# An RWKV time-mixing kernel: crossbar transposes from an earlier unit, 16 KB loads, another queue for the first weight, and output matmuls one unit later

## The chip, the cores and the metric

The kernel runs on one core of one Trainium2 chip. The metric is the device time of one execution in microseconds. The kernel before took 206.17 us (median of three, 205.88 to 206.23). Only fast runs (the granted TensorE clock at or near full speed over most of the run) are compared. A ratio is the mean time of one kernel's fast runs over the mean of the other kernel's fast runs in the same rounds, so it is not quite the ratio of the medians quoted.

## The reference

```python
# x: (16, 2048, 256) float32; x_prev is x shifted by one position
xv = x * time_mix_v + x_prev * (1 - time_mix_v)
xr = x * time_mix_r + x_prev * (1 - time_mix_r)
v = xv @ value_weight
r = xr @ receptance_weight
out = (sigmoid(r) * v) @ output_weight      # the key branch does not reach the output
```

## The kernel before

A batch is 2048 rows; a unit is 512 rows, four units to a batch, 64 in all. x is loaded as bf16 (GpSimd's queue casts on the way), transposed (on TensorE for units below 49, by the transposing DMA, the "crossbar", from 49 on), mixed with its shifted neighbour on VectorE, GpSimd and later ScalarE, projected twice, gated and projected again. The parts that matter:

```python
    LOOK = 6
    BYDMA = 3 * UB + 3                # units transposed by the crossbar (UB = 4)
    CROSS = NU - BYDMA - LOOK         # 43: the pass in which the crossbar starts
    FREE = CROSS                      # from here ScalarE takes part of the scaling
    LATE_O = CROSS                    # from here output matmuls run one unit later
    xpool  = ctx.enter_context(tc.tile_pool(name="xpool", bufs=6))
    opool  = ctx.enter_context(tc.tile_pool(name="opool", bufs=3))   # output, one tile per batch
    ...
    def load(b):
        ...
        return nc.gpsimd.dma_start(out=x_bf[b], in_=rows(b), max_dma_last_dim=8192)

    x_unit = opool.tile([P, 3, UJ, D], FP32, name="o_sb")     # first three units of x, float32
    ...
    for m, tm in enumerate([time_mix_r, time_mix_v]):
        nc.scalar.dma_start(...)                              # the two mix vectors
    for h in (1, 0):
        nc.sync.dma_start(...)                                # two halves of unit 0 of x
    nc.sync.dma_start(out=w_f32[:, 0], ...)                   # first weight
    nc.sync.dma_start(out=x_unit[:, 1], ...)
    ...
    nc.gpsimd.tensor_copy(out=x_bf3[:, 0, 0:1], in_=w_f32[:, 0, 0, 0:1])   # a gate: loads wait for the weight
    ...
    def output(g, z):
        b, e = divmod(g, UB)
        if e == 0:
            o_sb[b] = opool.tile([P, J, D], FP32, name="o_sb")
        ...
        nc.scalar.copy(out=o_sb[b][:, j0 : j0 + UJ, :], in_=ps)
        if b < BYUNIT:
            if e % 2 == 1:
                nc.sync.dma_start(out=unit_rows(out, b, e - 1, 2), ...)    # two units, 4 KB runs
        elif e % 2 == 1:
            store(nc.sync, b, j0 - UJ, j0 + UJ)                            # two units, 8 KB runs
```

In the traces psum_r and psum_v are TensorE's result tiles of the two projections, psum_o that of the output matmuls, and ps_t that of the transposes; xt is the transposed x, s_sb the sigmoid, z_sb the gated product. Each of the first three has a single buffer.

There are three output tiles, and the first of them holds x at the start; so batch 4 writes into the tile of batch 1 and must wait until batch 1's stores have landed. And the loads of batches 2 to 6 are all issued ahead in the first 32 us, so many loads stand in GpSimd's DMA queue when the first stores are issued.

Of the kernel before, what the change touches and what calls it, by code (L numbers as in the profile page):

```python
# [15 lines left out]
def kernel(  # L16
# [25 lines left out]
    nc = tc.nc  # L42

    B, S, D = x.shape
    P = 128
    KO = D // P
    J = S // P
    UJ = 4
    TU = UJ * P
    UB = J // UJ  # L50
# [1 line left out]
    LOOK = 6  # L52
    BYUNIT = 2
    H = UJ // 2
    BYDMA = 3 * UB + 3
    CROSS = NU - BYDMA - LOOK
    FREE = CROSS
    LATE_O = CROSS
    START_T = [1, 3, 5, 6, 7, 9, 11, 12]
    AHEAD = 6  # L60
    PAIRS = 10
# [18 lines left out]
    x_bf = {}  # L80
# [12 lines left out]
    def rows(b):  # L93
        return x[b].rearrange("(p j) d -> p j d", p=P)

    def unit_rows(t, b, e, n=1):

        return t[b, e * TU : (e + n) * TU, :].rearrange("(e p j) d -> p e j d", p=P, j=UJ)

    def load(b):  # L100
        if b not in x_bf:
            x_bf[b] = xpool.tile([P, J, D], BF16, name="x_bf")
        if b < BYUNIT:
            for e in range(UB):
                nc.gpsimd.dma_start(  # L105
                    out=x_bf[b][:, e * UJ : (e + 1) * UJ, :], in_=unit_rows(x, b, e)[:, 0]
                )
            return
        return nc.gpsimd.dma_start(out=x_bf[b], in_=rows(b), max_dma_last_dim=8192)  # L109

    x_unit = opool.tile([P, 3, UJ, D], FP32, name="o_sb")
    tm_rows = consts.tile([2 * KO, P], FP32)
    w_f32 = consts.tile([P, 2, KO, D], FP32)
    for m, tm in enumerate([time_mix_r, time_mix_v]):
        nc.scalar.dma_start(
            out=tm_rows[m * KO : (m + 1) * KO, :], in_=tm.rearrange("(ko p) -> ko p", p=P)
        )
    for h in (1, 0):
        nc.sync.dma_start(
            out=x_unit[:, 0, h * H : (h + 1) * H], in_=unit_rows(x, 0, 0)[:, 0, h * H : (h + 1) * H, :]  # L120
        )
    nc.sync.dma_start(
        out=w_f32[:, 0], in_=receptance_weight.rearrange("(ko p) n -> p ko n", p=P)
    )
    nc.sync.dma_start(out=x_unit[:, 1], in_=unit_rows(x, 0, 1)[:, 0])
    nc.sync.dma_start(out=w_f32[:, 1], in_=value_weight.rearrange("(ko p) n -> p ko n", p=P))
    sig0 = consts.tile([P, 1], BF16)
# [4 lines left out]
    x_bf3 = consts.tile([P, UJ, D], BF16)  # L132
    nc.gpsimd.tensor_copy(out=x_unit[:, 2, 0, 0:1], in_=x_unit[:, 0, 0, 0:1])
    nc.sync.dma_start(out=x_unit[:, 2], in_=unit_rows(x, 0, 2)[:, 0])
    nc.gpsimd.tensor_copy(out=x_bf3[:, 0, 0:1], in_=w_f32[:, 0, 0, 0:1])
    nc.gpsimd.dma_start(out=x_bf3, in_=unit_rows(x, 0, 3)[:, 0])
    nc.gpsimd.dma_start(out=wo_bf, in_=output_weight.rearrange("(ko p) n -> p ko n", p=P))
    load(1)
# [40 lines left out]
    def by_dma(b, lo, hi, after=None):  # L179

        op = nc.sync.dma_start_transpose(
            out=xt[b][:, 1 + lo : 1 + hi].rearrange("p j k c -> p (j k) c"),
            in_=x_bf[b][:, lo:hi].rearrange("p j d -> p (j d)"),
        )
        if after is not None:
            tc.add_manual_dep(op.ins, after.ins.name, SYNC, reason="not beside a load")

    def transposes(i):

        b, e = divmod(i, UB)  # L190
        if b > 0 and e == 0:
            new_xt(b)
        if b >= BYUNIT:
            e = (e - 1) % UB
        j0 = 1 + e * UJ + (e if b < BYUNIT else 0)
        if b < BYUNIT or e == UB - 1:
            late_copies.append((b, e))

        def one(ps, jj, ko, src, idn):
            nc.tensor.transpose(  # L200
                out=ps[:, jj], in_=src[:, jj, ko * P : (ko + 1) * P], identity=idn
            )

        if i in (1, 2):
            for ko in range(KO):
                ps = ps_t_pool.tile([P, UJ, P], FP32, name="ps_t")
                for jj in range(UJ):
                    one(ps, jj, ko, x_unit[:, i], ident_f)
                nc.scalar.copy(out=xt[b][:, j0 : j0 + UJ, ko, :], in_=ps)
            return  # L210
        ps = ps_t_pool.tile([P, UJ, KO, P], BF16, name="ps_t")
        src = x_bf3 if b == 0 else x_bf[b][:, e * UJ : (e + 1) * UJ, :]
        for jj in range(UJ):
            for ko in range(KO):
                one(ps[:, :, ko], jj, ko, src, ident)
        nc.scalar.copy(out=xt[b][:, j0 : j0 + UJ], in_=ps)  # L216
# [70 lines left out]
    def project_unmixed(ps, mo):  # L287


        parts = [(w_prev[:, ko], ko, 0) for ko in range(KO)]  # L290
        parts += [(w_bf[:, 0, ko], ko, 1) for ko in range(KO)]
        for n, (w, ko, lo) in enumerate(parts):
            nc.tensor.matmul(
                out=ps[:, mo, :],
                lhsT=w[:, mo * P : (mo + 1) * P],
                rhs=xt[0][:, lo : lo + UJ, ko],
                start=(n == 0),
                stop=(n == len(parts) - 1),
            )
# [86 lines left out]
    def pieces(g):  # L386

        b, e = divmod(g, UB)
        tile_for(g // 2)
        return [(b, m, e * TU, (e + 1) * TU) for m in range(2)]  # L390
# [22 lines left out]
    last_load = None  # L413

    def advance(limit):
        nonlocal tnext, last_load
        while tnext <= min(limit, NU - 1):
            b, e = divmod(tnext, UB)
            if b == 1 and e > 0:
                load(b + e + 1)  # L420
            elif b > 1 and e == 0 and b + 5 < B:
                if b == 2:
                    load(6)
                last_load = load(b + 5)
            if tnext < NU - BYDMA:
                transposes(tnext)
            tnext += 1

    first_transposes()
    for ko in range(KO):  # L430
        nc.vector.tensor_scalar(
            out=w_prev[:, ko, :],
# [6 lines left out]
        out=w_bf[:, 0, 0, :], in0=w_f32[:, 0, 0, :], scalar1=tms[:, 0, 0:1], scalar2=None, op0=ALU.mult  # L439
    )  # L440
    nc.scalar.activation(
        out=w_bf[:, 0, 1, :], in_=w_f32[:, 0, 1, :], func=ACT.Copy, scale=tms[:, 0, 1:2]
# [3 lines left out]
    for ko in range(KO):  # L446
        nc.vector.tensor_scalar(
            out=w_bf[:, 1, ko, :],
# [50 lines left out]
    shifted = None  # L499
    for g in range(NU - 1):  # L500
        ps_r = ps_r_pool.tile([P, KO, TU], FP32, name="psum_r")
        if g == 0:
            project_unmixed(ps_r, 0)
            advance(1)
            project_unmixed(ps_r, 1)
            for ko in range(KO):
                wrap_slots(pieces(1)[0], ko)
                scale(pieces(1)[0], (ko,))
            last = add(pieces(1)[0])
        else:  # L510
            project(ps_r, g, 0)
        s_sb = zpool.tile([P, KO, TU], BF16, name="s_sb")
        nc.scalar.activation(out=s_sb, in_=ps_r, func=ACT.Sigmoid)  # L513
        if g == CROSS:
            by_dma(B - 4, 0, 3 * UJ, last_load)
        advance(START_T[g] if g < len(START_T) else g + LOOK)
        for b in range(B - 3, B):
            if g == max(UB * (b - 2) - 1, CROSS):
                new_xt(b)
                by_dma(b, 0, J)  # L520
                shifted = b
        if LATE_O < g < NU - 2:
            output(g - 2, z_prev2)
        for p in products.get(g + 1, []):
            if g >= FREE and p[0][1] == 1:
                scale_act(p[0], (0,))
        for p in [q for q, _ in products[g]] + pooled[g]:
            last_unit_of = p[3] // TU - 1
            need = last_unit_of if p[0] < BYUNIT else min(last_unit_of + 1, UB - 1)
            assert UB * p[0] + need < tnext, (g, p, tnext)  # L530
            if g > AHEAD or p not in pooled[g]:
                wrap_slots(p)
        if g == 1:
            scale_act(pieces(2)[1], (1,))
        for p, kos in products[g]:
            if not (g - 1 >= FREE and p[1] == 1):
                scale(p, kos)
        for p in sums[g]:
            last = add(p)
        for p in pooled[g]:  # L540
            wrap_slots(p)
        ps_v = ps_v_pool.tile([P, KO, TU], FP32, name="psum_v")
        project(ps_v, g, 1)
        if g == 0:
            scale_act(pieces(1)[1], (0,))
            advance(2)
        z_sb = zpool.tile([P, KO, TU], BF16, name="z_sb")
        nc.vector.tensor_tensor(out=z_sb, in0=s_sb, in1=ps_v, op=ALU.mult)  # L548
        for p in pooled[g]:
            scale_pool(p, last)  # L550
        for p in held[g]:
            add(p)
        if z_prev is not None and not LATE_O <= g < NU - 3:
            output(g - 1, z_prev)
        if g == 1:
            advance(4)
        if shifted is not None and g == max(UB * (shifted - 2), CROSS + 1):
            nc.sync.dma_start(
                out=xt[shifted][:, 0, :, 1:P], in_=xt[shifted][:, J, :, 0 : P - 1]
            )  # L560
        z_prev2, z_prev = z_prev, z_sb
# [31 lines left out]
```

## Time and profile before

| | kernel before |
|---|---|
| time, median of 3 | 206.17 us |
| busy share: TensorE, VectorE, ScalarE, GpSimd | 97%, 93%, 88%, 41% |
| a unit while TensorE transposes / with the crossbar | 3.045 / 2.60 us |
| stores of 1 MB, issue to landing (median) | 9.8 us |
| x loads, issue to landing (median) | 27.6 us |

A busy share is an average over stages. Here the start (to 32.7 us) is bound by VectorE and the rest by TensorE, which the chain of waits tells and the shares don't.

### The profile page before, as it was taken

To read this page: it belongs to the slowest core of one execution; us is meant where nothing else is said; L and a number is where in the kernel's file an instruction comes from. 1 tells how busy PE (TensorE), PEld (TensorE's weight loads), DVE (VectorE), ACT (ScalarE), POOL (GpSimd) and SP (SyncE) were. 2 spreads that over 40 slices of the span, in tenths; PEclk is the share of its full clock that TensorE was granted. 3 is DMA by queue.
4 is the path that set the end of the run, shared out by engine and by line. 5 is a ranking of instruction groups with operands and counts; after the bars stand their busy time and mean duration, and the time that the engine had idled before them with its cause. 6 is when DMAs were issued, how large, how long until landed. Compare 5 with 4: busy or idle time off the path is not lost.

```text
span 203.9 us, 3968 instructions
## 1 busy us (share of the span) xinstructions
PE 197.0 (97%) x1460; PEld 127.9 (63%) x1460; DVE 188.9 (93%) x304; ACT 180.1 (88%) x199; POOL 84.3 (41%) x109
## 2 busy tenths in 40 slices
PE   8999999999999999999999999999999999999991
PEld 7666666666666666666666666666554556555570
DVE  3899999999999999999999999999999999999961
ACT  2799899999999999999999999999797899998981
POOL 1853624264434436344254534334434444444200
PEclk9999999999999999999999999999999999999999
DMA  5999999999999999999999999944896997999875
GB/s 176 288 184 218 244 276 277 276 281 277 305 312 310 316 308 305 293 295 304 304 302 284 296 297 298 341 174 188 259 197 123 297 290 254 230 397 412 350 287 193
DMA packets 28811, 56.15 MB, mean 275 GB/s; under 512 B 17396, under 2 KB 18680, under 8 KB 25720
## 3 DMA queue, kind: packets, MB, share of 16 engines
q1 hardware_dynamic: 23840, 39.65, 55.1%
q0 software_dynamic: 4800, 16.12, 40.0%
q8 instruction: 11, 0.18, 0.3%
q10 hardware_dynamic: 152, 0.13, 0.2%
q14 instruction: 8, 0.07, 0.1%
HBM read 34.34 MB, written 33.55 MB: 333 GB/s over the span
## 4 chain that ended last, share of the span: by engine, by line
PE 71%; DVE 11%; issue 6%; ACT 5%; POOL 3%; DMA 2%; SPq 0%; DVEq 0%; ACTq 0%
PE psum_r L279 21%; PE psum_v L279 21%; PE psum_o L303 20%; PE ps_t L200 8%; DVE mix L271 5%; DVE mix L249 3%; DVE z_sb L548 2%; ACT o_sb L335 2%; ACT s_sb L513 2%; DMA w_f<-n_receptance_weight_dram 2%; POOL x_bf L105 1%; ACT mix L491 1%; PE ps_t L303 1%; DVE xt_first L408 0%; PE ps_t L279 0%
## 5 line engine op out<-in xcount | busy, mean ns | idle before, releaser
L259 POOL TENSOR_SCALAR mix<-xt,c_sb 128x1024 bf16<-128x1024 bf16 (+1 forms) x55 | 62.0, 1127 | 93.0 <-DVE mix L271 85.6
L271 DVE TENSOR_TENSOR mix<-mix,xt 128x1024 bf16<-128x1024 bf16 x112 | 78.6, 708 | 1.9
L548 DVE TENSOR_TENSOR z_sb<-s_sb,psum_v 128x1024 bf16<-128x1024 bf16 x63 | 76.6, 1217 | 3.2 <-PE psum_v L279 1.6
L279 PEld LDWEIGHTS <-w_bf 128*128 128x128 bf16 x516 | 48.4, 98 | 38.6 <-DVE mix L271 1.5
L513 ACT ACTIVATE s_sb<-psum_r 128x1024 bf16<-128x1024 f32 x63 | 65.0, 1031 | 6.1 <-PE psum_r L279 5.8
L335 ACT COPY o_sb<-psum_o 128x1024 f32<-128x1024 f32 x60 | 61.1, 1018 | 7.7 <-PE psum_o L303 7.6
L279 PE MATMUL psum_v<-mix,w_bf 128*128 128x512 bf16 (+1 forms) x256 | 65.3, 377 | 0.5 <-DVE z_sb L548 0.2
L279 PE MATMUL psum_r<-mix,w_bf 128*128 128x512 bf16 (+1 forms) x252 | 64.3, 377 | 0.7 <-ACT o_sb L335 0.4
L303 PE MATMUL psum_o<-wo_bf,z_sb 128*128 128x256 bf16 x494 | 64.4, 273 | 0.1
L303 PEld LDWEIGHTS <-z_sb 128*128 128x128 bf16 x512 | 49.9, 98 | 20.1 <-DVE z_sb L364 0.8
L216 ACT COPY xt<-ps_t 128x1024 bf16<-128x1024 bf16 x41 | 41.6, 1026 | 0.0
L200 PEld LDWEIGHTS <-x_bf 128*128 128x128 bf16 x368 | 24.1, 98 | 10.3 <-POOL xt_first L407 0.6
L200 PE MATMUL ps_t<-ident,x_bf 128*128 128x128 bf16 x368 | 27.6, 219 | 0.1
L249 DVE TENSOR_SCALAR mix<-xt,c_sb 128x1024 bf16<-128x1024 bf16 (+1 forms) x52 | 23.5, 459 | 0.1
L109 POOL DMA_DIRECT2D x_bf<-in_x_dram x14 | 10.5, 751 | 0.0
L491 ACT ACTIVATE mix<-xt,c_sb 128x1024 bf16<-128x1024 bf16 x9 | 10.4, 1161 | 0.0
L271 DVE TENSOR_TENSOR mix<-mix,xt_first 128x1024 bf16<-128x1024 bf16 x15 | 10.2, 686 | 0.1
L259 POOL TENSOR_SCALAR mix<-xt_first,c_sb 128x512 bf16<-128x512 bf16 x6 | 4.1, 688 | 8.3 <-DVE xt_first L408 8.2
L249 DVE TENSOR_SCALAR mix<-xt_first,c_sb 128x512 bf16<-128x512 bf16 x22 | 6.7, 357 | 0.2
L216 ACT COPY xt_first<-ps_t 128x1024 bf16<-128x1024 bf16 x5 | 5.1, 1027 | 0.0
L144 PE MATMUL ps_t<-zeros 128*128 128x128 bf16 x31 | 3.4, 295 | 1.0 <-DVE zeros L87 1.0
L144 PEld LDWEIGHTS <-zeros 128*128 128x128 bf16 x31 | 3.1, 141 | 1.0 <-DVE zeros L87 1.0
(63 smaller groups left out, 46.6 us busy)
## 6 DMA issues: line engine op xcount, KB each, us to landing
out_dram<-o_sb SPq DMA_DIRECT2D x28, 1024.0 KB, 9.8
x_bf<-in_x_dram POOLq DMA_DIRECT2D x14, 1024.0 KB, 27.6
out_dram<-o_sb SPq DMA_DIRECT2D x4, 512.0 KB, 5.8
out_dram<-o_sb SPq DMA_DIRECT2D x6, 256.0 KB, 2.1
x_bf<-in_x_dram POOLq DMA_DIRECT2D x5, 256.0 KB, 7.0
o_sb<-in_x_dram SPq DMA_DIRECT2D x2, 512.0 KB, 4.7
o_sb<-in_x_dram SPq DMA_DIRECT2D x2, 256.0 KB, 2.9
out_dram<-o_sb SPq DMA_DIRECT2D x3, 128.0 KB, 2.0
```

Source lines behind the costliest of these rows:

```text
L109: return nc.gpsimd.dma_start(out=x_bf[b], in_=rows(b), max_dma_last_dim=8192)
L200: nc.tensor.transpose(out=ps[:, jj], in_=src[:, jj, ko * P : (ko + 1) * P], identity=idn)
L216: nc.scalar.copy(out=xt[b][:, j0 : j0 + UJ], in_=ps)
L249: nc.vector.tensor_scalar(out=mixed(piece)[:, :, ko], in0=xt[b][:, slots(piece), ko], scalar1=c_sb[:, m, ko : ko + 1], scalar2=None, op0=A ...
L259: op = nc.gpsimd.tensor_scalar(out=mixed(piece)[:, :, 1], in0=xt[b][:, slots(piece), 1], scalar1=c_sb[:, m, 1:2], scalar2=1.0, op0=ALU.mul ...
L271: return nc.vector.tensor_tensor(out=mixed(piece), in0=mixed(piece), in1=xt[b][:, slots(piece, 1)], op=ALU.add)
L279: nc.tensor.matmul(out=ps[:, mo, :], lhsT=w_bf[:, m, ko, mo * P : (mo + 1) * P], rhs=mixed((b, m, e * TU + lo, e * TU + hi))[:, :, ko], st ...
L303: nc.tensor.matmul(out=ps[:, slot, :], lhsT=z[:, ko, jj * P : (jj + 1) * P], rhs=wo_bf[:, ko, :], start=(ko == 0), stop=(ko == KO - 1),)
L335: nc.scalar.copy(out=o_sb[b][:, j0 : j0 + UJ, :], in_=ps)
L491: nc.scalar.activation(out=mixed(piece)[:, :, ko], in_=xt[b][:, slots(piece), ko], func=ACT.Copy, scale=c_sb[:, m, ko : ko + 1],)
L513: nc.scalar.activation(out=s_sb, in_=ps_r, func=ACT.Sigmoid)
L548: nc.vector.tensor_tensor(out=z_sb, in0=s_sb, in1=ps_v, op=ALU.mult)
```

## The change

Its intent: move three more units' transposes from TensorE to the crossbar; fill the hole that the moved output matmuls left; make loads cheaper to issue with 16 KB descriptors; bring the first weight in beside x, on another queue.

```diff
-    BYDMA = 3 * UB + 3
+    BYDMA = 4 * UB + 2
-    LATE_O = CROSS
+    LATE_O = CROSS - 1
@@ load @@
-        return nc.gpsimd.dma_start(out=x_bf[b], in_=rows(b), max_dma_last_dim=8192)
+        return nc.gpsimd.dma_start(out=x_bf[b], in_=rows(b), max_dma_last_dim=16384)
@@ start @@
+    nc.scalar.dma_start(out=w_f32[:, 0], in_=receptance_weight...)   # before the mix vectors
-    nc.sync.dma_start(out=w_f32[:, 0], in_=receptance_weight...)
-    nc.gpsimd.tensor_copy(out=x_bf3[:, 0, 0:1], in_=w_f32[:, 0, 0, 0:1])
+    nc.gpsimd.tensor_copy(out=x_bf3[:, 0, 0:1], in_=x_unit[:, 1, 0, 0:1])
@@ main loop @@
-            by_dma(B - 4, 0, 3 * UJ, last_load)
+            by_dma(B - 5, 1 * UJ, 3 * UJ, last_load)
-        for b in range(B - 3, B):
-            if g == max(UB * (b - 2) - 1, CROSS):
+        for b in range(B - 4, B):
+            if g == max(UB * (b - 2) - 1, CROSS + 1):
-        if shifted is not None and g == max(UB * (shifted - 2), CROSS + 1):
+        if shifted is not None and g == max(UB * (shifted - 2), CROSS + 2):
```

More of the change, by code (lines that the diff above doesn't have):

```diff
@@ L113 @@
     w_f32 = consts.tile([P, 2, KO, D], FP32)
+    nc.scalar.dma_start(
+        out=w_f32[:, 0], in_=receptance_weight.rearrange("(ko p) n -> p ko n", p=P)
+    )
     for m, tm in enumerate([time_mix_r, time_mix_v]):
@@ L121 @@
         )
-    nc.sync.dma_start(
-        out=w_f32[:, 0], in_=receptance_weight.rearrange("(ko p) n -> p ko n", p=P)
-    )
     nc.sync.dma_start(out=x_unit[:, 1], in_=unit_rows(x, 0, 1)[:, 0])
```

## The prediction

> **What bounds the kernel now.** A unit is 512 rows; there are 64, four to a batch, and pass g of the main loop computes the projections of unit g. I read the page first (TensorE 97% busy, VectorE 93%, ScalarE 88%, clock at full speed), then the chain of waits in order of time, then each engine's timeline where the change bites: 0 to 12 us and 134 to 204 us.
>
> The chain has three stretches. It opens with the first weight's transfer, runs over GpSimd's issue of x loads to VectorE, stays on VectorE to 32.7 us, and from there is TensorE. VectorE has no idle time between 11.4 and 31.5 us, so a later start there is a later end, one for one:
>
> ```profile
> 1.66 3.74 DMA w_f<-n_receptance_weight_dram
> 5.96 0.77 POOL x_bf L136
> ...
> 7.45 2.27 POOL x_bf L105 x4
> ...
> 10.52 0.69 POOL mix L259
> 11.37 0.68 DVE mix L271
> ...
> 31.52 1.14 DVE z_sb L548
> 32.70 1.02 PE psum_v L279 x4
> ```
>
> The timeline of TensorE shows the rhythm around unit 43, from which the crossbar takes over the transposing:
>
> ```profile
> 138.47 1.03 PE L279 MATMUL psum_r<-mix,w_bf 128*128 128x512 bf16 x4
> 139.33 0.61 PE L200 MATMUL ps_t<-ident,x_bf 128*128 128x128 bf16 x8
> 139.78 1.03 PE L279 MATMUL psum_v<-mix,w_bf 128*128 128x512 bf16 x4
> 140.64 1.04 PE L303 MATMUL psum_o<-wo_bf,z_sb 128*128 128x256 bf16 x8
> 141.51 1.03 PE L279 MATMUL psum_r<-mix,w_bf 128*128 128x512 bf16 x4
> 142.38 1.03 PE L279 MATMUL psum_v<-mix,w_bf 128*128 128x512 bf16 x4
> 143.70 1.02 PE L279 MATMUL psum_r<-mix,w_bf 128*128 128x512 bf16 x4 [0.30 <-ACT s_sb L513]
> ...
> 154.76 1.04 PE L279 MATMUL psum_r<-mix,w_bf 128*128 128x512 bf16 x4 [0.39 <-ACT o_sb L335]
> ```
>
> Read starts, not durations, which overlap. psum_r to psum_r is 141.51 - 138.47 = 3.04 us with the eight transposes (139.33 to 139.78, 0.45) and 2.60 later without (143.70 to 146.30). At 141.51 the output matmuls are left out so that from there they run one unit later; without them unit 44's psum_r waits for the sigmoid that empties its bank: 143.70 rather than 143.24, 0.46 lost. 143.70 + 4 x 2.60 = 154.10, but unit 48 starts at 154.76: 0.66 lost. Two more small losses follow: unit 50 at 160.17 (0.2) and unit 60 at 186.47 (0.27).
>
> Those last three come from the crossbar, as the queue of SyncE shows:
>
> ```profile
> 143.27 10.97 SPq L181 DMA_TRANSPOSE xt<-x_bf  x2
> 156.14 0.71 SPq L558 DMA_DIRECT2D xt<-xt  x1
> 156.95 0.54 SPq L313 DMA_DIRECT2D out_dram<-o_sb  x1
> 157.67 7.15 SPq L181 DMA_TRANSPOSE xt<-x_bf  x1
> ...
> 168.43 0.62 SPq L558 DMA_DIRECT2D xt<-xt  x1
> ...
> 169.81 7.14 SPq L181 DMA_TRANSPOSE xt<-x_bf  x1
> ```
>
> An issue holds the queue until its data has nearly gone; the shift copy (L558) then waits for landing, and stores wait behind both. A batch issued with no store ahead held it 4.88 us, with one 7.15. GpSimd shows who waits: its multiply for units 48 and 49, normally about 3.0 us after psum_r of unit 45 (149.3), came at 151.16, and the one for 60 and 61 waited for the last shift copy:
>
> ```profile
> 151.16 3.00 POOL L259 TENSOR_SCALAR mix<-xt,c_sb 128x1024 bf16<-128x1024 bf16 x2 [3.17 <-DVE mix L271]
> ...
> 181.77 1.12 POOL L259 TENSOR_SCALAR mix<-xt,c_sb 128x1024 bf16<-128x1024 bf16 x1 [1.69 <-DMA xt<-xt]
> ```
>
> **What the Trainium skill says.** "TensorE: Matmul & The Clock Gate", part 1, gives N / 2.4 GHz + 2.5 ns from start to start when warm: 8 x 55.8 = 0.45 us for a unit's transposes, which is what the trace has. "Advanced Engine Details and Errata", X-Bar Transpose (TRN2), calls transposing transfers as fast as plain ones, 350 to 400 GB/s; the trace disagrees: 1 MB in 4.88 us is 215 GB/s, against about 400 for stores late in the kernel. "DMA: Bandwidth & Descriptors", Queues, rings and completion order, says that each engine consumes a ring in order and takes turns between rings packet by packet; and Issuing engines are not separate DMA queues, that another issuing engine saves only issue time. No overlap of two hardware queues at the start exists in the trace of before to test that.
>
> **The change, part by part.**
>
> *Crossbar from 46.* CROSS goes from 43 to 40. TensorE loses 3 x 8 transposes: 3 x 0.445 = 1.33 us, all on the path, since TensorE is the chain there. ScalarE loses three copies of 1.03 us and takes, with FREE at 40, two multiplies of 1.16 us that VectorE had at 0.48. VectorE needs that: in the late stretch its z product, two adds and alternate multiply fill 5.2 of 5.2 us per pair of units, as TensorE does. Twelve slots of 64 KB are added to the crossbar, 12/16 x 4.88 = 3.7 us of transfers, beside other work: the transfer engines are 0.2 to 0.3 busy from 134 to 138 us and 0.06 from 140 to 142. VectorE's wrap copy for batch 12 becomes a fourth shift copy.
>
> *Output later, with LATE_O = CROSS - 1.* Unit 39 now skips the output while it still transposes unit 45; those 0.445 us fill the hole behind the sigmoid. So from psum_r of 39 to that of 44: before 4 x 3.045 + 2.19 = 14.37; after 2.17 + 4 x 2.60 = 12.58. Together with the first part 1.79 saved (1.33 and 0.46).
>
> *Earlier crossbar against need.* On before's clock the new starts are 129.3 (unit 39), 131.5 (40), then 2.60 each. The store of 36 and 37 leaves SyncE at about 131; the first issue (eight slots, 2.4 us plus that store's 2.5) runs to 136, batch 12 to 141, its shift lands near 146, needed at 144.5 + 3.0 = 147.5. Batch 13 lands near 156, needed 157.9; 14 near 167.7, needed 168.3; 15 near 178.2, needed 178.7. If so the losses of 0.66, 0.2 and 0.27 vanish: 1.13. The last two margins are half a microsecond, below my accuracy, so I give back 0.4.
>
> *16 KB descriptors.* Fourteen loads have half as many packets; GpSimd's issue should fall from 0.75 us towards the 0.57 of the loads with 128 descriptors. GpSimd is 41% busy: nothing on the path. The last load must have landed before the first crossbar issue; in before the transfer engines fall from 412 to 82 GB/s at 134, so it lands near 133, two us later than SyncE is ready. Larger packets give the loads a bigger share against stores, so I expect it a few us earlier. Worth 0 directly, but it protects the line above.
>
> *First weight on ScalarE's queue.* This I expect to cost. Before, the two mix vectors went first on ScalarE's queue and had landed before warm-up ended; TensorE takes its instructions in order, so the sequence below could start at 3.35:
>
> ```profile
> 1.31 0.24 ACTq L115 DMA_DIRECT2D tm_rows<-in_time_mix_v_dram  x1
> 3.35 0.26 PE L162 MATMUL psum_o<-ident_f,tm_rows 4*128 4x4 f32 x1
> ...
> 6.28 0.59 PE L293 MATMUL psum_r<-xt_first,w_prev 128*128 128x512 bf16 x2
> ```
>
> After, both vectors stand behind 256 KB of weight in the same rings, which take turns with the halves of x on SyncE's: 16 packets of 1 KB per engine against 2 x 8 of 2 KB, so weight and second half end together, after 768 KB. Before, transfers start near 1.9 us at 320 to 340 GB/s; 0.79 MB takes 2.3 us, and a landing is seen 0.9 us after its last bytes (weight: 4.5 by summing the windows, 5.40 in the chain). So vectors, weight and second half land near 5.1, not 3.2, 5.4 and 4.3. TensorE's first transposes and all behind them move by 5.1 - 3.35 = 1.7 us. GpSimd's gate moves too, from the weight (5.40) to the second x unit (about 7.0), hence its first multiply from 10.52 to about 11.8; that is inside the same delay. If the rings overlap better the delay is 0.5 to 1; I take 1.2.
>
> Sum: 206.17 - 1.79 - 1.13 + 0.4 + 1.2 = 204.9.
>
> **Rivals.** (a) The start is not hurt, because two queues keep the engines fuller: the windows show 209 to 307 GB/s at 3.5 to 5.5 us while the weight goes, against about 400 at 6 to 7.5. The second x unit lands a little sooner and nothing is lost: 203.3 to 203.6. Against it: the order within a ring. (b) The crossbar becomes the bound. A full cycle on SyncE took 12.1 us (157.67 to 169.81) and TensorE eats a batch in 10.4; four cycles must now fit instead of three, and if the last load is late all slip. The stalls come back, 1 to 2.5 us: about 206.5. For it: the margins of 0.5 us; against it: 13 to 14 took only 8.3. (c) VectorE is the bound once transposes are gone, as its late stretch has no idle time: the saved 1.33 shrinks to about 0.8. Against it: in 162 to 180 us TensorE keeps 2.60 exactly.
>
> **Range and chances.** Best case is the full saving with no lost start, 203.2. Worst is the start at +1.7 and stalls as in (b), about 206.6. A 2% gain needs 202.0, below anything that I can add up; a 2% loss needs 210.3, for which several of these must fail together.
>
> **What would show it.** Right: the 41 ScalarE copies from ps_t to xt become 38; psum_r of 39 to 44 in 12.6 us; no idle gap of TensorE near units 44 and 48; the coefficient transpose L162 at 4.5 to 5.3 and the first projection (6.28 before) 1 to 1.7 us later. Wrong: L162 still near 3.4, so that the start costs nothing; shift copies landing after GpSimd's turn for batches 14 and 15; or steps above 2.65 us from unit 40 on, which would put VectorE in TensorE's place.

## More of the kernel before

One reading that the prediction did not take belongs here: the transfer queues between 25 and 45 us, when loads and stores both have work waiting. The columns are packets, MB written, and the share of the 16 engines' time; q0 carries GpSimd's loads, q1 SyncE's stores. The third line is the list of transfers from 15 to 75 us (number, size, median us from issue to landing); the fourth is ScalarE's first copy into batch 4's tile, which did not wait for a store.

```profile
q0 software_dynamic: 720, 2.76, 67.9%
q1 hardware_dynamic: 717, 2.79, 36.8%
...
out_dram<-o_sb SPq DMA_DIRECT2D x9, 1024.0 KB, 13.4
...
65.55 1.01 ACT L335 COPY o_sb<-psum_o 128x1024 f32<-128x1024 f32 x1 [0.20 <-PE psum_o L303]
```

The queues took turns, packet for packet: 720 against 717. The share of bytes is then a matter of packet size. The stores of batches 0 and 1, which fill this stretch, go out in 4 KB runs, the later ones in 8 KB runs (420 packets for 3.05 MB from 60 to 75 us), so the first stores have the smaller turn.

## The result, and the profile after

The changed kernel took 212.85 us (six runs, 212.19 to 213.2) against 206.07 us (six runs, 205.4 to 206.57): ratio 1.0327, interval 1.0302 to 1.0351. It is 3% slower, where the prediction had 203.2 to 206.6 us.

Stepping through both traces by the start of psum_r of given units tells where it went:

| stretch | before | after | difference |
|---|---|---|---|
| to unit 10 | 40.97 us | 43.12 us | +2.15 |
| unit 10 to 39 | 88.35 | 96.26 | +7.91 |
| unit 39 to 44 | 14.38 | 13.19 | -1.19 |
| unit 44 to 48 | 11.06 | 10.62 | -0.44 |
| unit 48 to 60 | 31.71 | 31.20 | -0.51 |

The parts that were to gain did gain (2.14 us), the start lost somewhat more than the 1.7 us worked out, and 7.9 us appeared in a stretch that the prediction left alone. The chain of waits of the changed kernel (start, duration, what) shows what it was:

```profile
40.39 1.07 ACT o_sb L335
41.48 32.15 DMA out_dram<-o_sb
73.73 1.02 ACT o_sb L335
74.79 1.86 PE psum_o L303 x8
76.66 1.71 PE psum_r L279 x4
```

One store of 1 MB, issued at 41.48 us, landed 32.15 us later. It is the second half of batch 1; the copy that waited for it is the first of batch 4, which gets the same tile. The timelines of ScalarE and TensorE (in brackets the idle time before and what ended it):

```profile
73.73 1.01 ACT L335 COPY o_sb<-psum_o 128x1024 f32<-128x1024 f32 x1 [6.24 <-DMA out_dram<-o_sb]
...
74.79 1.86 PE L303 MATMUL psum_o<-wo_bf,z_sb 128*128 128x256 bf16 x8 [4.97 <-ACT o_sb L335]
```

ScalarE took its instructions in order: the sigmoid of unit 18, whose psum_r was done at 68.5 us, ran only at 74.64, behind the blocked copy, and the next transpose copy behind that. TensorE had no free psum_o tile (the pool has one): it stood 4.97 us. Then it came back slowly. These are views by stretch (length, then busy us and instructions of PE, PEld, DVE, ACT and POOL, then the granted clock, the DMA share and GB/s); the first line is the kernel before, the others the changed one:

```profile
69.00:75.00 6.00, 6.00 (x49) 4.00 (x48) 5.64 (x9) 5.59 (x7) 2.24 (x2) 1.00 1.05 315
...
69.80:74.80 5.00, 0.03 (x2) 0.01 (x1) 0.01 (x1) 1.07 (x2) 1.11 (x1) 0.89 1.02 278
74.80:77.80 3.00, 3.00 (x12) 1.64 (x12) 2.10 (x3) 2.78 (x3) 0.00 (x0) 0.50 1.05 281
77.80:80.60 2.80, 2.80 (x14) 1.52 (x13) 0.81 (x2) 1.93 (x2) 1.12 (x1) 0.52 0.98 322
80.60:86.60 6.00, 6.00 (x49) 4.01 (x48) 5.38 (x9) 4.71 (x6) 1.12 (x1) 1.00 1.01 427
```

From 74.8 to 80.6 us TensorE had half its clock; psum_r to psum_r took 5.04 us there (76.45 to 81.49) rather than 3.05. So of the 7.9 us, 5.9 fell in the pass that stood (psum_r at 67.49 to 76.45, 8.96 - 3.05) and 2.0 in the pass after it. The standstill itself is 5.0; the other 2.9 fit the half clock, which lasted 5.8 us.

Why did the store take so long? The queues from 25 to 45 us and the stores from 15 to 75 us, the answer to the lines shown for before:

```profile
q0 software_dynamic: 456, 3.34, 79.9%
q1 hardware_dynamic: 452, 1.79, 23.4%
...
out_dram<-o_sb SPq DMA_DIRECT2D x8, 1024.0 KB, 24.5
```

The turns are still one for one, 456 against 452, but a load's turn is longer. From these rows a load packet took 0.799 x 16 engines x 20 us / 456 = 0.56 us of an engine (before: 0.679 x 320 / 720 = 0.30), a store packet 0.17 (before 0.16). A pair of turns thus takes 0.73 us rather than 0.47, and in 20 us the stores got 1.79 MB out rather than 2.79. In this stretch of the changed kernel, three stores of 1.05 MB were issued within 20 us, 0.16 MB/us, and 0.09 MB/us left. The stores fell behind for as long as loads were queued. The engines were busy nearly all the time in both kernels (shares of 105 and 103%, as packets overlap); counting a load twice, as it reads float32 and writes bf16, 2 x 2.76 + 2.79 = 8.3 MB went through before and 2 x 3.34 + 1.79 = 8.5 MB after. Over this stretch nothing was lost in throughput; it was given to the wrong queue.

At the start, the timeline answers the lines shown in the prediction:

```profile
1.84 0.25 ACTq L118 DMA_DIRECT2D tm_rows<-in_time_mix_v_dram  x1
...
5.14 0.24 PE L162 MATMUL psum_o<-ident_f,tm_rows 4*128 4x4 f32 x1 [1.74 <-DMA tm_rows<-in_time_mix_v_dram]
...
8.14 0.94 PE L293 MATMUL psum_r<-xt_first,w_prev 128*128 128x512 bf16 x2
```

The mix vectors, behind the weight in their ring, landed at 5.1 us, and the first projection began at 8.14, not 6.28. TensorE took its work in order here: the first half-unit of x landed at about 4.0 us (issued at 0.74, 3.3 us to land), but its transposes began at 5.31, behind L162.

Around the start of the crossbar:

```profile
139.38 1.03 PE L279 MATMUL psum_r<-mix,w_bf 128*128 128x512 bf16 x4
140.24 0.61 PE L200 MATMUL ps_t<-ident,x_bf 128*128 128x128 bf16 x8
140.69 1.03 PE L279 MATMUL psum_v<-mix,w_bf 128*128 128x512 bf16 x4
141.57 1.02 PE L279 MATMUL psum_r<-mix,w_bf 128*128 128x512 bf16 x4
...
151.71 1.02 PE L279 MATMUL psum_v<-mix,w_bf 128*128 128x512 bf16 x4 [0.21 <-DVE z_sb L548]
```

Unit 39 without output takes 2.19 us with its transposes inside it, so the hole is filled as expected; but from unit 40 to 44 it is 152.57 - 141.57 = 11.0 us where four times 2.60 is 10.4. TensorE waits for VectorE at 151.71, and VectorE had been held by GpSimd, whose multiply came late. This trace puts that wait down to TensorE; that it was for the first crossbar data is taken from e3's trace and tested by e11.

### The profile page after: what moved, and what is told of

Read it like the earlier page. It is cut to its first block, busy times and chain, and to the rows that moved or that the text cites. A ratio compares the mean times of both kernels' runs of the same rounds, so it can differ in the third digit from the quotient of the medians.

```text
span 211.3 us, 3923 instructions
## 1 busy us (share of the span) xinstructions
PE 198.9 (94%) x1436; PEld 128.4 (61%) x1436; DVE 187.4 (89%) x301; ACT 179.2 (85%) x198; POOL 80.0 (38%) x109
## 4 chain that ended last, share of the span: by engine, by line
PE 55%; DMA 17%; DVE 14%; ACT 6%; issue 5%; ACTq 1%; POOL 0%; DVEq 0%; POOLq 0%
PE psum_v L279 16%; PE psum_r L279 16%; PE psum_o L303 15%; DMA out_dram<-o_sb 15%; DVE mix L271 6%; PE ps_t L200 5%; DVE z_sb L548 4%; DVE mix L249 3%; ACT o_sb L335 3%; ACT s_sb L513 2%; DMA tm_rows<-in_time_mix_v_dram 1%; ACT xt L216 1%; DVE xt_first L408 1%; PE psum_r L293 1%; PE ps_t L144 1%
## 5 line engine op out<-in xcount | busy, mean ns | idle before, releaser
L259 POOL TENSOR_SCALAR mix<-xt,c_sb 128x1024 bf16<-128x1024 bf16 (+1 forms) x55 | 61.0, 1109 | 102.1 <-DVE mix L271 96.5
L271 DVE TENSOR_TENSOR mix<-mix,xt 128x1024 bf16<-128x1024 bf16 x112 | 77.8, 703 | 1.7
L303 PE MATMUL psum_o<-wo_bf,z_sb 128*128 128x256 bf16 x494 | 65.2, 275 | 5.1 <-ACT o_sb L335 5.0
L279 PE MATMUL psum_r<-mix,w_bf 128*128 128x512 bf16 (+1 forms) x252 | 65.1, 381 | 0.1
L216 ACT COPY xt<-ps_t 128x1024 bf16<-128x1024 bf16 x38 | 38.6, 1029 | 0.0
L200 PEld LDWEIGHTS <-x_bf 128*128 128x128 bf16 x344 | 23.0, 99 | 9.5 <-issue 0.6
L200 PE MATMUL ps_t<-ident,x_bf 128*128 128x128 bf16 x344 | 26.2, 221 | 0.0
L249 DVE TENSOR_SCALAR mix<-xt,c_sb 128x1024 bf16<-128x1024 bf16 (+1 forms) x50 | 22.5, 457 | 0.0
L491 ACT ACTIVATE mix<-xt,c_sb 128x1024 bf16<-128x1024 bf16 x11 | 12.8, 1161 | 0.0
L109 POOL DMA_DIRECT2D x_bf<-in_x_dram x14 | 8.1, 577 | 0.0
```

What stands on the lines that cost most here:

```text
L200: nc.tensor.transpose(out=ps[:, jj], in_=src[:, jj, ko * P : (ko + 1) * P], identity=idn)
L216: nc.scalar.copy(out=xt[b][:, j0 : j0 + UJ], in_=ps)
L249: nc.vector.tensor_scalar(out=mixed(piece)[:, :, ko], in0=xt[b][:, slots(piece), ko], scalar1=c_sb[:, m, ko : ko + 1], scalar2=None, op0=A ...
L259: op = nc.gpsimd.tensor_scalar(out=mixed(piece)[:, :, 1], in0=xt[b][:, slots(piece), 1], scalar1=c_sb[:, m, 1:2], scalar2=1.0, op0=ALU.mul ...
L271: return nc.vector.tensor_tensor(out=mixed(piece), in0=mixed(piece), in1=xt[b][:, slots(piece, 1)], op=ALU.add)
L279: nc.tensor.matmul(out=ps[:, mo, :], lhsT=w_bf[:, m, ko, mo * P : (mo + 1) * P], rhs=mixed((b, m, e * TU + lo, e * TU + hi))[:, :, ko], st ...
```

## The experiments

The theory after reading the traces, A: the 16 KB loads take turns that are twice as long, stores starve, and the three output tiles run out. Its rivals: B, the later start makes the burst of loads meet the first stores; C, the crossbar part costs the time; D, large descriptors lower throughput as such; E, any 16 KB load starves the stores, burst or not. Eight runs took the change apart, four tested what is left. All twelve results were correct.

**e1_16k_only**: the kernel before with one line changed.

```diff
-max_dma_last_dim=8192
+max_dma_last_dim=16384
```

> The kernel before with the 16 KB descriptors alone. Theory A (the large loads starve the stores): a store of batch 1 lands only after some 30 us, ScalarE waits for its buffer near 68 us, TensorE stands 5 us and then runs some 6 us at half clock; time 206.1 + 7.9 = 214 us. Rival B (the starving needs the later start, which lets the burst of loads meet the first stores): no stall, 206 us. Rival C (the crossbar part costs the time): 206 us.

Measured: 213.42 us (before 206.17), ratio 1.0335 (1.0281 to 1.0388). Unit 10 to 39 took 94.95 us rather than 88.35, with ScalarE idle 6.0 us for a store and TensorE 4.77. The descriptors alone are the loss, with the old start and the old crossbar: B and C fall.

**e2_start_only**: the weight on ScalarE's queue and the gate on the second x unit, nothing else (the part of the diff marked "start").

> The kernel before with the first weight on ScalarE's queue and the gate on the second x unit, nothing else. From the two traces the transpose of the mix vectors moves from 3.35 to 5.1 us and VectorE's steady stretch from 11.37 to 13.6: 206.1 + 2.2 = 208.3 us, with no stall near 70 us. Rival B: the stall near 70 us appears here too: about 214 us.

Measured: 208.11 us, ratio 1.0085 (1.0042 to 1.0128). No stall: unit 10 to 39 took 88.35 us. The start costs about 1.9 us. The old start varies between runs (unit 10 began at 40.97 to 42.87 us in eight traces of kernels with it, 41.99 on average; at 43.12 to 44.34 in the five traces with the change's own order on ScalarE's queue, 43.86), so 1.9 is better founded than the 2.15 of the first pair. About 1.5 of it lies before the first projection (6.63 us on average with the old start, 8.10 with the new). The rest, and some of the spread, goes with TensorE's pace just after: a pair of the first projection's matmuls took 0.59 us in the kernel before and 1.06 in e2, but also in e3 and e11, which have the old start. The views by stretch record a clock of 1.00 there, so a slow clock is only inferred.

**e3_cross_only**: the crossbar and the output shift, 8 KB loads, old start.

> The kernel before with the crossbar from 46 on and the output one unit later, 8 KB descriptors and the old start. Theory A: this is the part that gains: 206.1 - 2.1 = 204.0 us as read from the two traces, or up to 1 us less gain because the last load, at 8 KB, lands near 133 us, 2 us after SyncE could issue the first transpose. Rival C: no gain or a loss, 206 us or more.

Measured: 204.42 us, ratio 0.9898 (0.9839 to 0.9958). From unit 39 to 60 the trace has 55.14 us against 57.15. This part gains about 2 us: 2.0 against this one trace of the kernel before, 1.8 against the 56.9 of the five traces e1, e2, e6, e7 and e14, which have the old crossbar part too. It falls short of its full sum, and GpSimd's wait for the first crossbar data shows where:

```profile
139.38 1.12 POOL L259 TENSOR_SCALAR mix<-xt,c_sb 128x1024 bf16<-128x1024 bf16 x1 [1.79 <-DMA xt<-x_bf]
```

**e4_after_8k**: the changed kernel with 8192 again.

> The changed kernel with the descriptors back at 8 KB. Theory A: stores land within 15 us as before, the stall near 70 us is gone, 212.85 - 7.9 = 205 us, to 206 if the last load is late for the crossbar. Rival B or C: 212 us still.

Measured: 206.2 us, ratio 0.9985 (0.9935 to 1.0035); unit 10 to 39 in 88.36 us. Taking the large descriptors out of the whole change gives back 6.6 us, so e1 and e4 agree from both sides. Of the rest, the start's loss and the crossbar's gain cancel.

**e5_after_4_out_bufs**: the changed kernel with a fourth output tile.

```diff
-tc.tile_pool(name="opool", bufs=3)
+tc.tile_pool(name="opool", bufs=4)
```

> The changed kernel, 16 KB descriptors and all, with a fourth output buffer. Theory A (the stall is a wait for an output buffer whose store the loads starve): the stores still take 24 to 32 us to land in the first third, but the batch that needs the buffer comes 12 us later, so no engine waits: 212.85 - 7.9 = 205 us. Rival D (large descriptors cost transfer throughput as such, so the work is late whatever the buffers): 210 us or more.

Measured: 205.5 us, ratio 0.9967 (0.9945 to 0.9989). The stores are as slow as in the changed kernel, here between 15 and 75 us:

```profile
out_dram<-o_sb SPq DMA_DIRECT2D x9, 1024.0 KB, 25.3
```

Yet nothing waits, and unit 10 to 39 takes 88.35 us. So D falls, and the damage is shown to need both: slow stores and a buffer that comes round too soon.

**e6_16k_late_loads**: the kernel before, 16 KB only for batches 7 to 15.

```diff
+max_dma_last_dim=16384 if b > 6 else 8192
```

> The kernel before with 16 KB descriptors only for batches 7 to 15, which are loaded after the first burst. Theory A, in the form that the burst of loads 2 to 6 queued in the first 35 us is needed to starve a store beyond its slack: no stall, 206 us (205.5 to 206.5), while the loads of the later batches land sooner than in the kernel before (10 to 16 us rather than 18 to 40). Rival E (any load at 16 KB starves a store beyond its slack): a stall, 210 us or more.

Measured: 206.58 us, ratio 1.0021 (0.9994 to 1.0048), no stall. Loads issued from 75 to 130 us landed in 13.7 us (23.9 before), stores in 17.9 us (9.6 before). So stores slow down here as well, but stay within their slack; E falls: without large descriptors in the first burst of loads there is no stall.

**e7_4k_loads**: the step in the other direction.

```diff
-max_dma_last_dim=8192
+max_dma_last_dim=4096
```

> The kernel before with 4 KB descriptors, the opposite step. If the engines share by packets in turn (theory A), stores land sooner in the first third, near 9 us where they took 13 at 8 KB and 25 at 16 KB, and loads land later, 35 us or more; the time stays at 206 us as neither is waited for. If packet size does not set the shares, landing times stay near 13 and 33 us.

Measured: 206.3 us, ratio 1.0014 (0.9987 to 1.0042). In the list for 15 to 75 us:

```profile
x_bf<-in_x_dram POOLq DMA_DIRECT2D x9, 1024.0 KB, 35.1
out_dram<-o_sb SPq DMA_DIRECT2D x9, 1024.0 KB, 8.7
```

Stores took 8.7 us at 4 KB, 13.4 at 8 KB and 29.1 at 16 KB (e1; 24.5 in the changed kernel); loads 35.1, 33.5 and 20.3 (18.9). Packet size moves the shares in the order that turn-taking asks for, and the time hardly notices until a buffer runs out. At 4 KB the turns over the whole stretch were not one for one (1308 load packets to 775 of stores from 25 to 45 us), because the store queue was empty for part of it. Windows of 1 us show this: from 31 to 32 us 50 load packets and 49 of stores, from 36 to 37 us 102 and 2, from 43 to 44 us 103 and none.

**e8_vectors_first**: the new start with the two vectors ahead of the weight on ScalarE's queue.

```diff
+    for m, tm in enumerate([time_mix_r, time_mix_v]):
+        nc.scalar.dma_start(...)
     nc.scalar.dma_start(out=w_f32[:, 0], ...)
-    for m, tm in enumerate([time_mix_r, time_mix_v]):
-        nc.scalar.dma_start(...)
```

> The new start, alone on the kernel before, with the two mix vectors ahead of the weight on ScalarE's queue. If the vectors' place behind the weight were all of the start's loss: 206.1 us. If the first half of x that now lands at 5.4 rather than 4.4 us is the rest of it (my theory), the transposes of that half start near 5.4 instead of 6.1: about 0.8 us of the 2.0 come back, 207.3 us.

Measured: 210.49 us (208.49 to 211.08), ratio 1.0189 (1.0127 to 1.0252): a miss, and slower than e2. The vectors were early and L162 ran at 3.40 us, but then the weight itself was awaited:

```profile
8.89 0.61 DVE L431 TENSOR_SCALAR w_prev<-w_f,tm_prev 128x256 bf16<-128x256 f32 x2 [3.75 <-DMA w_f<-n_receptance_weight_dram]
```

Issued 0.86 us later than in the change, the weight took 7.3 us to land. The half-unit of x that was awaited landed at 4.5, not at 5.4 as I had held. Turn-taking with the 4 KB packets of the second x unit, beside which the weight's are 1 KB, fits this, but the transfer rate was also lower (231 GB/s from 4.0 to 4.5 us, where e2 has 438), and why is open. TensorE then stood 2.6 us for the weight, and its granted clock was 0.50 to 0.58 from 10 to 13 us, which is likely part of why e8 is slower than e2. What follows is only that placing the weight on the second queue costs in either order.

**e14_start_gate_weight**: the new start with GpSimd's gate back on the weight.

```diff
-in_=x_unit[:, 1, 0, 0:1]
+in_=w_f32[:, 0, 0, 0:1]
```

> The new start alone, with GpSimd's gate back on the first weight. If the gate on the second x unit is inside the delay that the vectors cause, as I predicted: the same 208.1 us as the new start with it. If the gate is the cause: about 206.5 us.

Measured: 208.19 us, ratio 1.0085 (1.0054 to 1.0115), L162 at 5.14 us. As with e2; the gate is not the cause.

**e9_cross_no_late**: e3 with the output shift left at CROSS.

```diff
-    LATE_O = CROSS - 1
+    LATE_O = CROSS
```

> The crossbar part without the shift of the output matmuls by one unit (LATE_O stays at CROSS). My working of the prediction: the hole behind the sigmoid, 0.46 us, comes back, now at unit 40, so 0.46 us slower than the crossbar part with it (ratio 0.9898 to before), about 0.992, and the gap of psum_r of 39 to 44 is 0.4 to 0.5 us longer. Rival: the first crossbar issue is late by 0.6 us anyway and hides the hole: same as with it.

Measured: 204.41 us, ratio 0.9917 (0.9890 to 0.9943). From unit 39 to 44 it is 13.82 us against 13.01 in e3, 0.8 longer, but from 44 to 48 it is 0.38 shorter; over 39 to 60 the trace has 55.57 against 55.14. The shift is worth 0.43 us in the traces. The times alone, from another call and chip, cannot separate e3 from e9.

**e12_cross_16k_4_bufs**: e3 with 16 KB descriptors for all loads and a fourth output tile.

> The changed kernel with the old start and a fourth output buffer, so everything of the change that need not cost. Theory: no stall, the start of before, the crossbar's saving: 206.1 - 2.1 = 204.0 us, ratio 0.99. Rival D (large descriptors cost throughput): 205.5 us or more.

Measured: 203.51 us, ratio 0.9874 (0.9856 to 0.9893). Stores issued between 15 and 75 us took 31.2 us to land, and no engine waited for them.

**e11_cross_early**: e3, with 16 KB only for batches 7 to 15 and the first two crossbar issues earlier.

```diff
-        if g == CROSS:
-            by_dma(B - 5, 1 * UJ, 3 * UJ, last_load)
         advance(START_T[g] if g < len(START_T) else g + LOOK)
+        if g == CROSS - 2:
+            by_dma(B - 5, 1 * UJ, 3 * UJ, last_load)
-            if g == max(UB * (b - 2) - 1, CROSS + 1):
+            if g == max(UB * (b - 2) - 1, CROSS):
```

> The crossbar part with the old start, 16 KB descriptors for batches 7 to 15 only, and the first two crossbar issues earlier: batch 11 at unit 38, ahead of the store of units 36 and 37, batch 12 at unit 40. Theory: the two late arrivals left in the crossbar part (TensorE loses 0.6 us before unit 44 and 0.4 us before unit 48) vanish, so 0.8 to 1.0 us better than the crossbar part alone: ratio 0.985, 203 us. Rival: SyncE's in-order queue only moves the delay to batches 14 and 15, no gain: ratio 0.99.

Measured: 203.3 us, ratio 0.9864 (0.9837 to 0.9890). From unit 39 to 44 it took 12.61 us, where the prediction's sum was 12.58, and from 44 to 48 10.40, four times 2.60. The large descriptors for the late batches are not the reason: with 16 KB and the crossbar part's own order, e12 has 13.03 and 10.57. Both late arrivals are gone, and batches 14 and 15 are not delayed (31.20 us from 48 to 60). This version beats both kernels, by 1.4% over the one before; the saved time is also about all that this part has to give.

## Why the prediction was wrong

The predicted time was 204.9 us and the measured one 212.85. By its own steps:

- **16 KB descriptors, "Worth 0 directly": this step failed.** It said that larger packets "give the loads a bigger share against stores" and stopped there. The premise was right; the step not taken was to ask what becomes of the stores. It cost 6.6 to 7.9 us (e1, e4 and the traces). Nor was the crossbar any better protected by it: from unit 39 to 44 e3 took 13.01 us with 8 KB, e12 13.03 with 16 KB. Only the issue cost came as predicted (0.58 us a load). All numbers for the loss lay in the profile of before: packets in turn, 720 against 717; 0.30 us for a load's and 0.16 for a store's, so with doubled loads an estimated 0.30 x 2 + 0.16 = 0.76 us for a pair of turns, hence 16 engines x 4 KB / 0.76 us = 86 KB/us for the stores, against a production of two units, 1.05 MB, per 6.1 us, 172 KB/us. The measured 90 KB/us is close to it. But a rate below production is not yet a stall: before, 2.79 MB in 20 us was 140 KB/us, also below 172. What counts is how late the stores get against the slack. A tile comes round after two batches: in the kernel before, the fourth store was issued at 39.34 us and its tile was wanted at 65.55. At 86 KB/us the first four stores, 4.19 MB from 18.89 us on, would last to an estimated 67.5 us, after the need; at 140 KB/us to 48.8, well before it (it landed at 54.1). In the changed kernel the fourth store took 32 us, against a slack of 26.
- **The cold clock** was no term at all. A standstill of 5.0 us cost 2.9 us more at half clock, 2.0 of them in the pass after it.
- **First weight on ScalarE's queue: right mechanism, size taken wrongly.** The landings came as worked out (5.1 us), and the whole delay is 1.9 us (e2, e14) where the working had 1.7. The error is the cut to 1.2 for a better overlap of the rings. The two queues did move more (404 to 438 GB/s from 3.5 to 5.0 us in e2, where the kernel before has 209 to 307), but what the chain waited for was the last of what the two rings shared. That the gate lies "inside the same delay" is confirmed by e14.
- **Crossbar and output shift: right, but 0.4 to 0.7 us short.** Predicted 2.5 us net of the 0.4 given back, measured 2.14 in the changed kernel and 2.0 in e3 (1.8 against the five other traces). The prediction compares arrival with need for batches 12 to 15, but not for the first issue: the quarters of a batch are transposed in the order 3, 0, 1, 2, so batch 11's crossbar slots serve units 45 and 46, and GpSimd multiplies units 44 and 45 together, so it needs them at the turn of unit 41. e11, which issues earlier, gets the whole sum (54.21 us from unit 39 to 60 against 57.15).
- **Rivals.** (a) is refuted by e2. (b), a late crossbar, occurred at the first two issues (0.6 and 0.2 us in the changed kernel), not at batches 14 and 15 where I looked for it. The steps above 2.65 us that were to show (c) did appear (2.83 and 2.98 us at units 42 and 43), but (c) is refuted by e11: without late data TensorE keeps 2.60 us from unit 40 on.

Still open: why transfers were slower at the start in e8 than in e2, how much of the start's loss another order of the small transfers could give back, and whether larger descriptors for the first stores, which go out in 4 KB runs, would also have prevented the stall; no run gave them any.

## What to carry to other kernels

Where two DMA queues share the engines packet by packet, as they did here (456 turns to 452), a larger descriptor in one is a smaller share for the other: multiply the turns out before calling it free, and compare the share that the other queue keeps with what it must carry while both have work. Then find the buffer whose reuse waits for that queue, and work out when its store lands. A store that is late costs nothing until its tile comes round (e5: 25.3 us to land, no wait); here the copy that then waited held the sigmoid behind it, TensorE stood 5.0 us, and the half clock took 2.9 more. And where TensorE takes its work in order, the smallest transfer (two vectors of 1 KB) can set the start if it stands behind a large one (L162 at 5.14 us rather than 3.35).

## What the Trainium skill lacked or had wrong

- "DMA: Bandwidth & Descriptors", Queues, rings and completion order: it says that an engine drains a packet of typically 9 to 17 descriptors before it turns to another queue. Here the profile counted about one packet for each descriptor (3.8 KB written per load packet, so 7.7 KB read, at 8 KB) and the turns went one for one (720 to 717 at 8 KB, 456 to 452 at 16 KB), so byte shares follow the descriptor size. The page lacks that consequence: stores landed in 8.7, 13.4 and 29.1 us beside loads of 4, 8 and 16 KB (e7, before, e1).
- "DMA: Bandwidth & Descriptors", Rules for kernel authors, says that spreading DMAs over queues does not help bandwidth. At the start, with the weight and x on two queues, e2 moved 404 to 438 GB/s from 3.5 to 5.0 us, against 209 to 307 with both on one queue; but e8, also with two, moved 115 to 295, so no run here gives a rule.
- "Advanced Engine Details and Errata", X-Bar Transpose (TRN2): 350 to 400 GB/s stated; 1 MB held the queue for 4.88 us here, 215 GB/s, and the engines moved 218 GB/s from 152 to 155 us with only a transpose under way.
- "TensorE: Matmul & The Clock Gate", part 1, has about 3.4 us of sustained work before full speed returns, counted in windows that do not start with the work. After the 5 us standstill the granted clock stayed at 0.50 to 0.52 for 5.8 us of nearly unbroken matmuls. That is within two such windows (6.8 us, an estimate from the page's figure), so it does not contradict the page, but 3.4 us would have been too short an estimate of this wait.
